# Dilated attention in a two-layer encoder block: probabilities transposed in place, and scores placed behind the next projection

## The chip, the cores and the metric

The kernel runs on one core of one Trainium2 chip. The metric is the device time of one execution in microseconds; lower is better. A core has a matrix engine (TensorE, PE in the profile), three engines for elementwise work (VectorE = DVE, ScalarE = ACT, GpSimd = POOL), an engine that here only issues DMAs (SyncE = SP), 16 DMA engines, an on-chip memory of 128 partitions (SBUF) and a matrix accumulator of eight banks (PSUM).

## The reference, cut to what matters

One batch of 512 tokens, width 1024, float32, 16 heads of 64. Layer A is a dilated attention of three groups of heads (dilations 1, 4 and 16; each query sees 64, 64 and 16 keys of its residue class on either side), whose outputs are weighed by their softmax denominators; one softmax over all keys of the three groups is the same. Layer B is a neighbourhood attention on an 8 x 64 grid.

```python
def mixer_a(hn, w_in, w_out, q_gain, k_gain, t5_bias):
    proj = hn @ w_in
    qkv = proj[..., :n_qkv].reshape(b, s, 3, 3, N_HEADS, HEAD_DIM)
    gate = proj[..., n_qkv:]
    for g, (window, dilation) in enumerate(((128, 1), (512, 4), (2048, 16))):
        q = rms_norm(qkv[:, :, g, 0], q_gain[g])
        k = rms_norm(qkv[:, :, g, 1], k_gain[g])
        v = qkv[:, :, g, 2]
        o, lse = dilated_group_attention(q, k, v, t5_bias[g], dilation, (window // 2) // dilation)
    alpha = softmax(lses)
    y = sum(alpha * outs) * silu(gate)
    return y @ w_out

# per layer: x = x + mixer(rms_norm(x))
```

## The kernel before

**Tiling and stages.** `main()` runs, for each of eight pairs of heads of layer A (`hc` 0 to 7; the text calls the pairs heads 0 to 7), three projections: `rawk` (k of the groups 1 and 2, and their v), `rawq` (q of all groups and k of group 0), each 96 matmuls of 128 x 512, and the pair of `v0_a` and `gate_a` with 24 each. Head 7 takes `rawq` ahead of `rawk`, and the gate of head 6 comes behind them. Then come the output product of layer A, eight heads of layer B, and the output product of B. A float32 product is three products of rounded parts: weights are split by ACT into `wh` (L127) and by DVE or POOL into `wl` (L131; POOL takes two of five). Weights are loaded on SP's queue into three buffers `wraw`.

**Order.** The order of PE is written out by hand: `run(main(), side())` walks the projections (main) and lets the attention work (side) in between, by a clock that counts PE time. `yield "wait", key, delay` in the side work means: not before `delay` ns of that clock after the stamp `key`; `yield n` means n ns on; `later_on` sets a timer for DMAs. The order on the other engines, and that of DMAs not held by `keep_in_program_order`, is chosen by the scheduler of the framework, from its own estimate of times.

**A head of layer A.**
- `project_qk`: ACT evacuates each of four accumulators (L444, L468 for the first head), POOL squares (L268), DVE sums (L269), the norm's inverse root is computed in 14 small operations on POOL for `rawk` and 11 on DVE for `rawq` (`rsqrt`, L108 to L120), and DVE scales in place (L290). `rawq` is then transposed on DVE in 32 x 32 blocks (`turn_q`, L519).
- `k_a`: two groups of PE transposes of `rawk` (L505 and on).
- `q_a`: `rawq` goes to DRAM in four writes and comes back in four reads (k0, q0 and the two parts of q12), by timers at 0 and 6.8 us. The writes have rows of 512 bytes. Then `split_q` (L552) makes k0h (ACT, L559), q0h (ACT, L578), q0l (DVE, L580) and k0l (DVE, L561).
- `scores(u)`, in two halves u of two query tiles t each: per half four PSUM banks `log` (two tiles x two heads), out of a pool `side` of four. Group 0 is three products of 192 or 256 columns into the front half of a bank, the groups 1 and 2 are 64 small products into its back half.
- `softmax` (L741): per bank two sweeps of DVE that add the bias and keep the minimum (scores are negated): one over group 0 (L748), one over the groups 1 and 2 that starts from the first one's minimum (L759). Then ACT's exponential with the sum (L770), DVE's reciprocal (L608), ACT's scaling (L609), into a tile `p` of four buffers.
- `turner.put` (L681): DVE transposes p in 32 x 32 blocks into a tile `tr` of one buffer; `turner.send`: four writes to DRAM (L690) and four reads (L694) finish the transpose into `pq` ("pt" in the profile). Head 7 transposes on PE instead (`turn_p`, L774).
- `weigh`: the product with v (`o`, 24 matmuls), whose result is gated by `put_y` into y_h (ACT, L635) and y_l (POOL, L636).

**Where these stand on PE before.** The scores of a head 1 to 5 follow its own projections: first half, then (waiting for rawk of the next head) the product with v of the head before, and 10 us behind that rawk the second half. Head 0's halves wait for rawk and rawq of head 1. Head 6's follow each other by 11 us during rawq and rawk of head 7.

The lines that set these places:

```python
def k_a(hc):
    yield "wait", ("rawk", hc), 12500 if hc == 0 else 25500 if hc == 1 else 18500 if hc < NHC - 1 else 10000

def q_a(hc):
    yield "wait", ("rawq", hc), 15000 if hc != 1 else 18000

def land():
    yield "wait", ("rawq", hc), 27000 if hc != 1 else 30000
```

Of the kernel before, what the change touches and what calls it, by code (L numbers as in the profile page):

```python
# [42 lines left out]
def tile_hybrid_encoder(  # L43
# [45 lines left out]
    ones = cp.tile([P, S], F32R, name="ones")  # L89
# [176 lines left out]
    def squares(v, ss, i, ns):  # L266
        sq = wk.tile([P, 512], F32, tag="sq", name="sq")[:, : ns * 64]
        nc.gpsimd.tensor_mul(sq.rearrange("p (c r) -> p c r", r=32) if ns == 8 else sq, v, v)  # L268
# [6 lines left out]
    def head_norm(raw, ss, ns, held):  # L275
# [5 lines left out]
        def scale():  # L281
            for i in range(4):
                by = rs[:, i * ns : (i + 1) * ns].unsqueeze(2)
                if ns == 8:
                    v = raw[:, :, i, :].rearrange("p (a b) r -> p a b r", b=2)
                    by = by.unsqueeze(3).to_broadcast([P, ns, 2, 32])
# [62 lines left out]
    for _ in range(9):  # L349
        nc.tensor.matmul(busy, ones[:, :P], ones, start=True, stop=True)  # L350
# [61 lines left out]
    pq = wk.tile([P, 4096], F32, tag="pt", name="pt", bufs=1)  # L412
    rk = wk.tile([P, 4608], F32, tag="rawk", name="rawk", bufs=1)
# [4 lines left out]
    def project_qk(n, ns, key, hc, guard, first=False, **kw):  # L418
# [3 lines left out]
        def evac(i, acc):  # L422
# [11 lines left out]
            if key == "rawq":  # L434
                pieces = [(raw[:, :, i, :], acc.rearrange("p (c r) -> p c r", r=32))]
# [69 lines left out]
    def k_a(hc):  # L505
        yield "wait", ("rawk", hc), 12500 if hc == 0 else 25500 if hc == 1 else 18500 if hc < NHC - 1 else 10000
# [14 lines left out]
    def q_a(hc):  # L521

        yield "wait", ("rawq", hc), 15000 if hc != 1 else 18000
        raw = st.pop(("rawq", hc))
        d = dr.tile([16, 32, 4, P], F32, name="qd", tag="qd", bufs=2)
        q12 = wk.tile([P, 2, 512], F32, tag="q12", name="q12", bufs=1)
        k0, q0 = (wk.tile([P, 512], F32, tag="eg", name="q0") for _ in range(2))
        lands, left = ((3, k0), (0, q0), (1, q12[:, 0, :]), (2, q12[:, 1, :])), [4]

        def write(t):  # L530
            src = raw[32 * t : 32 * t + 32].rearrange("k c i r -> k c (i r)")
            tc.keep_in_program_order(nc.sync.dma_start(d[:, :, t, :].rearrange("c k x -> k c x"), src))
            if t == 3:
                stamp["q", hc] = 0

        def read(f, dst):
            src = d[4 * f : 4 * f + 4].rearrange("a k t x -> (a k) (t x)")
            tc.keep_in_program_order(nc.sync.dma_start(dst, src))
            left[0] -= 1

        for n in range(4):
            later_on(700 * n, partial(write, n))
            later_on(6800 + 700 * n, partial(read, *lands[n]))
        def land():
            yield "wait", ("rawq", hc), 27000 if hc != 1 else 30000
            assert not left[0]
            st["q", hc] = split_q(q0, k0, q12)
            yield
# [3 lines left out]
    def split_q(q0, k0, q12):  # L552
# [4 lines left out]
        src = k0.rearrange("p (t j r) -> p t r j", t=4, j=4)  # L557
        trj4 = lambda t: t[:, 64:EXT].rearrange("p (t r j) -> p t r j", t=4, j=4)
        nc.scalar.copy(trj4(k0h), src)  # L559
        put_k([(q0h, q0l, q0)], 0)  # L560
        nc.vector.tensor_sub(trj4(k0l), src, trj4(k0h.bitcast(F32)))  # L561
        return q0h, q0l, q12, k0h, k0l
# [107 lines left out]
    class turner:  # L670
# [3 lines left out]
        def __init__(self, run):  # L674
            self.run, self.left = run, 4
            self.t = wk.tile([P, 2048], F32, tag="tr", name="tr", bufs=1)
# [24 lines left out]
    def attn_a(hc):  # L701
        e0, e12 = st.pop(("e", hc))
        q0h, q0l, q12, k0h, k0l = st.pop(("q", hc))
# [5 lines left out]
        def scores(u):  # L709
# [13 lines left out]
            for t, lgs, cs, n in tiles:  # L723
                for g in range(2):
                    for j in range(4):
                        c = P * t + 32 * j
                        for hd in range(2):
# [3 lines left out]
                                q12[hs, g, c : c + 32],  # L731
# [8 lines left out]

        def softmax(hd, t, lg, cs, n):  # L741
            pr = wk.tile([P, 512], F32, tag="p", name="p", bufs=4)
            mn = wk.tile([P, 4], F32, tag="mn", name="mn", bufs=4)
            if t == 0:
                nc.gpsimd.memset(pr[:, 0:64], 0.0)
            if t == 3:
                nc.gpsimd.memset(pr[:, 192:256], BIG)
            nc.vector.tensor_tensor_reduce(  # L748
                out=pr[:, cs : cs + n],
                in0=lg[:, cs : cs + n],  # L750
                in1=e0[:, hd, cs : cs + n],
                scale=1.0,
                scalar=3.0e38,
                op0=ALU.add,
                op1=ALU.min,
                accum_out=mn[:, 0:1],
            )
            v = lambda t_: t_[:, 256:512].rearrange("p (g c) -> p g c", g=2)
            nc.vector.tensor_tensor_reduce(  # L759
                out=v(pr),  # L760
                in0=v(lg),
                in1=e12[:, 2 * hd : 2 * hd + 2, 96 - 32 * t : 224 - 32 * t],
                scale=1.0,
                scalar=mn[:, 0:1],
                op0=ALU.add,
                op1=ALU.min,
                accum_out=mn[:, 1:2],
            )
            row = pr[:, cs:512]
            nc.scalar.activation(row, row, AF.Exp, bias=mn[:, 1:2], scale=-1.0, accum_out=mn[:, 2:3])  # L770
            normalise(row, mn)
            return pr

        def turn_p(hd, t, pr):  # L774
            tp = bank("tp")
            for i in range(4):
                transpose(tp[:, i * P : (i + 1) * P], pr[:, i * P : (i + 1) * P])
# [3 lines left out]
        def weighed():  # L781

            yield "wait", ("rawk", hc + 1), 0
# [456 lines left out]
```

## Time and profile before

| what | value |
|---|---|
| time, median of 3 runs | 869.8 us (869.4 to 869.89) |
| the profiled execution | 867.95 us, of it 866.1 us span |
| TensorE (PE) | mean granted clock 0.992 of full speed |
| weights, activations and probabilities moved | 145.43 MB, mean 168 GB/s |

The page of the profile shows one execution: the busy time of each engine as a share of the span, the span in 40 slices, DMA queues, the chain of work that ended last, and the costliest groups of instructions. Further views of the same trace are used: the list of waits (engine, line, what released it: total us, times, longest), timelines (start, duration, engine, line, operation, out<-in, form; in brackets the idle time before it and what ended it), windows (engine busy times in a stretch of the span, then clock, DMA share and GB/s) and groups of instructions of one form (busy us, mean ns | idle before). For groups of operations such as "x64", one row stands for several instructions in a run.

### The profile page before, as it was taken

Reading aid. Unit: us, or ns where it says so; the run is one execution under the profiler, and the core shown is the slowest. Engines: PE = TensorE matmul, PEld = TensorE weight load, DVE = VectorE, ACT = ScalarE, POOL = GpSimd, SP = SyncE. Lnnn points to the kernel's source line nnn. Section 1 sums busy time; section 2 is a strip of 40 time slices with the busy share of each in tenths; the row PEclk is TensorE's granted clock in tenths of the full one; section 3 lists DMA queues with packets and bytes.
Section 4 is the critical chain, followed back from the end, with each engine's and each line's share of the span. In section 5 each row is a group of like instructions: output and inputs, shape, how many; then the busy total and the mean of one; then the engine's idle time right before and its main releaser. Section 6 shows DMA issues by size and latency. Waiting matters only on the chain.

```text
span 866.1 us, 15411 instructions
## 1 busy us (share of the span) xinstructions
PE 845.2 (98%) x5515; PEld 702.3 (81%) x5515; DVE 520.8 (60%) x1339; ACT 433.1 (50%) x924; POOL 304.9 (35%) x493
## 2 busy tenths in 40 slices
PE   9999998999999999999998988999999999999998
PEld 7788886788787788788787876789988999889786
DVE  7355583765674665665664855538576656766643
ACT  7434552653553553553553464436366545665541
POOL 2342432441541541541542332111444345533511
PEclk9999999899999999999999999999999999999999
DMA  6355468379478479478469196255235654556223
GB/s 246 111 158 175 147 190 232 133 204 231 139 209 241 139 193 239 137 203 231 138 173 262 49 256 183 64 180 194 80 119 155 172 169 147 153 165 182 98 91 128
DMA packets 81212, 145.43 MB, mean 168 GB/s; under 512 B 7408, under 2 KB 41136, under 8 KB 81136
## 3 DMA queue, kind: packets, MB, share of 16 engines
q1 hardware_dynamic: 80848, 144.44, 56.7%
q8 instruction: 43, 0.70, 0.4%
q14 instruction: 33, 0.27, 0.1%
q10 hardware_dynamic: 288, 0.01, 0.0%
HBM read 111.20 MB, written 33.22 MB: 167 GB/s over the span
## 4 chain that ended last, share of the span: by engine, by line
PE 76%; DMA 9%; DVE 5%; ACT 4%; POOL 3%; issue 1%; SPq 1%; ACTq 0%; DVEq 0%; POOLq 0%
PE acc L206 64%; PE log L206 4%; PE o L206 4%; DMA wraw<-in_w 3%; DMA q<-qd 3%; PE tp L210 3%; DMA qd<-rawq 1%; DMA e<-l_d 1%; POOL wl L131 1%; POOL sq L268 1%; DVE rawq L519 1%; DVE rawq L290 1%; DMA pt<-td 1%; ACT wh L127 1%; ACT rawq L444 1%
## 5 line engine op out<-in xcount | busy, mean ns | idle before, releaser
L206 PE MATMUL acc<-wh,hn_h 128*128 128x512 f32 (+1 forms) x768 | 293.3, 382 | 4.4 <-ACT rawq L444 2.4
L127 ACT CAST wh<-wraw 128x512 fp32r<-128x512 f32 (+1 forms) x276 | 161.1, 589 | 251.4 <-PE acc L206 190.8
L206 PE MATMUL acc<-wl,hn_h 128*128 128x512 f32 (+1 forms) x768 | 285.4, 372 | 0.6 <-DVE wl L131 0.6
L206 PE MATMUL acc<-wh,hn_l 128*128 128x512 f32 (+1 forms) x768 | 285.6, 372 | 0.0
L131 POOL TENSOR_TENSOR wl<-wraw,wh 128x512 fp32r<-128x512 f32 (+1 forms) x110 | 141.1, 1283 | 389.5 <-ACT wh L127 367.2
L131 DVE TENSOR_TENSOR wl<-wraw,wh 128x512 fp32r<-128x512 f32 (+1 forms) x166 | 116.8, 704 | 116.2 <-ACT wh L127 111.9
L206 PEld LDWEIGHTS acc<-wh,hn_h 128*128 128x128 f32 x768 | 144.4, 188 | 33.4 <-issue 4.0
L206 PEld LDWEIGHTS acc<-wh,hn_l 128*128 128x128 f32 x768 | 144.3, 188 | 20.6
L206 PEld LDWEIGHTS acc<-wl,hn_h 128*128 128x128 f32 x768 | 144.5, 188 | 20.0 <-DVE wl L131 0.9
L206 PE MATMUL acc<-hn_h,wh 128*128 128x512 f32 x192 | 78.6, 409 | 2.6 <-ACT rawk L444 2.3
L206 PE MATMUL acc<-hn_l,wh 128*128 128x512 f32 x192 | 75.8, 395 | 0.0
L206 PE MATMUL acc<-hn_h,wl 128*128 128x512 f32 x192 | 75.8, 395 | 0.0
L770 ACT ACTIVATE p<-p,mn 128x512 f32<-128x512 f32 (+1 forms) x64 | 45.1, 705 | 59.9 <-DVE mn L759 59.9
L609 ACT ACTIVATE p<-p,mn 128x512 f32<-128x512 f32 (+3 forms) x128 | 69.4, 593 | 2.9 <-DVE mn L608 2.9
L269 DVE TENSOR_REDUCE ss<-sq 128x4 f32<-128x256 f32 (+1 forms) x96 | 48.4, 505 | 29.2 <-POOL sq L268 28.7
L268 POOL TENSOR_TENSOR sq<-rawk 128x256 f32<-128x256 f32 x64 | 42.7, 675 | 64.9 <-ACT rawk L444 51.9
L681 DVE STREAM_TRANSPOSE tr<-p 128x512 f32<-128x512 f32 (+1 forms) x80 | 53.7, 683 | 10.4 <-ACT p L609 6.2
L206 PE MATMUL acc<-y_h,wh 128*128 128x512 f32 x128 | 52.2, 408 | 0.0
L206 PE MATMUL acc<-y_h,wl 128*128 128x512 f32 x128 | 50.0, 391 | 0.0
L206 PE MATMUL acc<-y_l,wh 128*128 128x512 f32 x128 | 50.0, 390 | 0.0
L206 PEld LDWEIGHTS acc<-hn_h,wh 128*128 128x128 f32 x192 | 36.9, 192 | 13.0 <-ACT rawk L444 4.9
L206 PEld LDWEIGHTS acc<-hn_h,wl 128*128 128x128 f32 x192 | 36.6, 191 | 8.0
(130 smaller groups left out, 1075.8 us busy)
## 6 DMA issues: line engine op xcount, KB each, us to landing
wraw<-in_w SPq DMA_DIRECT2D x95, 512.0 KB
wraw<-in_w SPq DMA_DIRECT2D x38, 384.0 KB
td<-tr SPq DMA_DIRECT2D x56, 256.0 KB
pt<-td SPq DMA_DIRECT2D x56, 256.0 KB
qd<-rawq SPq DMA_DIRECT2D x32, 256.0 KB
q<-qd SPq DMA_DIRECT2D x32, 256.0 KB
td<-tr SPq DMA_DIRECT2D x24, 224.0 KB
pt<-td SPq DMA_DIRECT2D x24, 224.0 KB
```

What stands on the lines that cost most here:

```text
L127: nc.scalar.copy(h, raw)
L131: eng.tensor_sub(l, raw, h.bitcast(F32))
L206: nc.tensor.matmul(o, l, r, **kw)
L210: nc.tensor.transpose(o, i, ident)
L268: nc.gpsimd.tensor_mul(sq.rearrange("p (c r) -> p c r", r=32) if ns == 8 else sq, v, v)
L269: nc.vector.tensor_reduce(ss[:, i * ns : (i + 1) * ns], sq.rearrange("p (a b) -> p a b", b=64), axis=AX.X, op=ALU.add)
L290: m = nc.vector.tensor_mul(v, v, by)
L444: nc.scalar.activation(dst, src, AF.Copy, scale=rs_n[:, i : i + 1])
L519: nc.vector.transpose(raw[:, :, i, :], raw[:, :, i, :])
L609: nc.scalar.activation(pr, pr, AF.Copy, scale=mn[:, 3:4])
L681: nc.vector.transpose(dst, src[:, :n].rearrange("p (i b k) -> p i b k", b=4, k=32))
L770: nc.scalar.activation(row, row, AF.Exp, bias=mn[:, 1:2], scale=-1.0, accum_out=mn[:, 2:3])
```

## The change

What it does, by parts:

1. **Softmax and transposition.** A tile `uu` of 4096 columns replaces `p` and `tr`. `spot` gives every (head, t) its place in it, each half of the scores its own 2048 columns, for heads 0 to 6 ("far") already laid out as the DRAM writes want it. The sweeps write there: four of 128 columns per bank (group 0 in two pieces, groups 1 and 2), each starting from the minimum so far, in place of two. Masked corners of tiles 0 and 3 are set to a large number, so that the exponential runs over all 512 columns. DVE transposes p where it lies, and `turner.send` writes from `uu`. Layer B takes slots of `uu` in turn.
2. **Order on PE.** The scores of heads 0 to 6 wait for the end of the next head's first projection; then come `split_q`, the pending product with v, the first half 1.2 us later and the second half 4.5 us of projection behind that. The functions for the old places go.
3. **q.** `rawq` is kept in another order of its 32-column blocks, so that the DRAM writes have rows of 2 KB, and the reads bring one quarter of the partitions each, all groups at once, into one tile `qt`. The waits of `k_a`, `q_a` and `land` are 19.5, 15.5 and 28 us. k0h is held in program order.
4. **Warm-up.** `ones` is two columns wide and broadcast.

```diff
-    ones = cp.tile([P, S], F32R, name="ones")
+    ones = cp.tile([P, 2], F32R, name="ones")
...
+    uu = wk.tile([P, 4096], F32, tag="uu", name="uu", bufs=1)
+    p_slots = cycle(range(4))
+    def p_slot():
+        o = 512 * next(p_slots)
+        return uu[:, o : o + 512]
...
-                pieces = [(raw[:, :, i, :], acc.rearrange("p (c r) -> p c r", r=32))]
+                src = acc.rearrange("p (f a r) -> p f a r", f=4, a=4)
+                pieces = [(raw[:, :, i, :].rearrange("p (a f) r -> p f a r", a=4), src)]
...
-        yield "wait", ("rawk", hc), 12500 if hc == 0 else 25500 if hc == 1 else 18500 if hc < NHC - 1 else 10000
+        yield "wait", ("rawk", hc), 12500 if hc == 0 else 19500 if hc < NHC - 1 else 10000
...
-        yield "wait", ("rawq", hc), 15000 if hc != 1 else 18000
+        yield "wait", ("rawq", hc), 15500
...
+        d = dr.tile([4, P, 512], F32, name="qd", tag="qd", bufs=2)
+        qt = wk.tile([P, 4, 4, P], F32, tag="q12", name="qt", bufs=1)
...
+        def write(a):
+            src = raw[:, 4 * a : 4 * a + 4].rearrange("p f i r -> p (f i r)")
+            tc.keep_in_program_order(nc.sync.dma_start(d[a], src))
...
+        def read(a):
+            dst = qt[32 * a : 32 * a + 32].rearrange("k t f x -> k t (f x)")
+            src = d[a].rearrange("(t k) x -> k t x", t=4)
+            tc.keep_in_program_order(nc.sync.dma_start(dst, src))
...
-            yield "wait", ("rawq", hc), 27000 if hc != 1 else 30000
+            yield "wait", ("rawq", hc), 28000
...
-        nc.scalar.copy(trj4(k0h), src)
-        put_k([(q0h, q0l, q0)], 0)
+        tc.keep_in_program_order(nc.scalar.copy(trj4(k0h), src))
+        by_t = lambda t: t.rearrange("p (t x) -> p t x", t=4)
+        put_k([(by_t(q0h), by_t(q0l), qt[:, :, 0, :])], 0)
...
+        far = hc < NHC - 1
+        def spot(hd, t):
+            o = 256 * hd + 128 * (t % 2) if far else 1024 * (t % 2) + 512 * hd
+            return 2048 * (t // 2) + o, *((32, 512) if far else (128, 32))
...
         def softmax(hd, t, lg, cs, n):
-            pr = wk.tile([P, 512], F32, tag="p", name="p", bufs=4)
...
+            least = 3.0e38
+            for i in range(4):
+                b, nb = {(0, 0): (2, 2), (3, 1): (0, 2)}.get((t, i), (0, 4))
+                c, w = P * i + 32 * b, 32 * nb
+                by = e0[:, hd, c : c + w] if i < 2 else e12[:, 2 * hd + i - 2, 96 - 32 * t : 224 - 32 * t]
+                bk = lambda t_: t_.rearrange("p (b k) -> p b k", k=32)
+                nc.vector.tensor_tensor_reduce(
+                    out=sb(uu, o + i_ * i + b_ * b, [[b_, nb], [1, 32]]),
+                    in0=bk(lg[:, c : c + w]),
+                    in1=bk(by),
+                    scale=1.0,
+                    scalar=least,
+                    op0=ALU.add,
+                    op1=ALU.min,
+                    accum_out=mn[:, i : i + 1],
+                )
+                least = mn[:, i : i + 1]
+            row = sb(uu, o, [[512, 4], [1, 128]] if far else [[1, 512]])
+            nc.scalar.activation(row, row, AF.Exp, bias=least, scale=-1.0, accum_out=mn[:, 4:5])
+            normalise(row, mn[:, 2:6])
...
             for u in range(2):
-                if u == 0 and hc:
-                    yield 600
-                elif hc == 0:
-                    yield "wait", ("rawk" if u == 0 else "rawq", 1), 0
-                elif hc < NHC - 2:
-                    yield "wait", ("rawk", hc + 1), 10000
-                else:
-                    yield 11000
-                turned = turner(512)
+                yield 1200 if u == 0 else 4500
+                turned = turner(uu[:, 2048 * u : 2048 * u + 2048], 512)
                 turners.append(turned)
                 for hd, t, pr in scores(u):
-                    turned.put(pr, 512, 256 * hd + 128 * (t % 2))
-                later_on(7500, partial(turned.send, pq[:, 2048 * u : 2048 * u + 2048], 11000, 1500))
-                if 0 < hc < NHC - 2 and u == 0:
-                    yield from weighed()
+                    nc.vector.transpose(pr, pr)
+                later_on(9500, partial(turned.send, pq[:, 2048 * u : 2048 * u + 2048], 11000, 1500))
...
-                if hc == NHC - 2:
-                    yield "wait", ("rawq", hc + 1), 0
+
+                follow = ("rawk" if hc < NHC - 2 else "rawq"), hc + 1
+                yield "wait", follow, 0
+                yield from st.pop(("land", hc))
+                if pending:
                     pending.pop(0)()
-                yield from chain(st.pop(("land", hc)), attn_a(hc))
+                yield from attn_a(hc)
```

More of the change, by code (lines that the diff above doesn't have):

```diff
@@ L349, in tile_hybrid_encoder @@
     for _ in range(9):
-        nc.tensor.matmul(busy, ones[:, :P], ones, start=True, stop=True)
+        wide = lambda n: ones[:, 0:1].to_broadcast([P, n])
+        nc.tensor.matmul(busy, wide(P), wide(S), start=True, stop=True)
     wsteps = steps()
@@ L702, in attn_a @@
         e0, e12 = st.pop(("e", hc))
-        q0h, q0l, q12, k0h, k0l = st.pop(("q", hc))
+        q0h, q0l, qt, k0h, k0l = st.pop(("q", hc))
         k12, v12 = st.pop(("k12", hc))
@@ L744, in softmax @@
             if t == 0:
[L745 removed]
+                nc.gpsimd.memset(sb(uu, o, [[b_, 2], [1, 32]]), BIG)
             if t == 3:
[L747 to L770, printed above, removed]
@@ L778, in turn_p @@
             dst = sb(pts[0], at(t, 0, hd, 0), [[32, 4], [512, 4], [1, 32]])
             nc.vector.tensor_copy(dst, tp.rearrange("p (i a r) -> p i a r", i=4, a=4))
-        def weighed():
-            yield "wait", ("rawk", hc + 1), 0
-            pending.pop(0)()
-            yield
         def weigh():
@@ L830, in attn_a @@
             for u in range(2):
-                if u == 0:
-                    yield "wait", ("gate", hc), 500
                 yield 600
@@ L836, in attn_a @@
                 if pending:
-                    yield "wait", ("gate", hc - 1), 16800
+                    yield "wait", ("gate", hc - 1), 15500
                     pending.pop(0)()
@@ L1006, in softmax @@
         def softmax(hd, u, lg):
-            pr = wk.tile([P, 512], F32, tag="p", name="p", bufs=4)
+            pr = p_slot()
             for b in (2 * u, 2 * u + 1):
```

63 lines of the change are left out of this document (30 added, 33 removed).

## The prediction

> **What bounds the kernel now.** I read the page first: the busy shares of the engines, then the list of what TensorE (PE) waited for.
>
> ```profile
> span 866.1 us, 15411 instructions
> PE 845.2 (98%) x5515; PEld 702.3 (81%) x5515; DVE 520.8 (60%) x1339; ACT 433.1 (50%) x924; POOL 304.9 (35%) x493
> ```
>
> ```profile
> PE log L206 <- ACT q0h L578: 4.2, 1, 4.2
> PE tp L210 <- DVE rawk L290: 3.1, 1, 3.1
> PE acc L206 <- ACT rawq L444: 2.4, 1, 2.4
> PE acc L206 <- ACT rawk L444: 2.3, 1, 2.3
> PE acc L206 <- ACT gt L478: 1.8, 2, 1.6
> ```
>
> PE is busy for 98% of the span and its matmuls are the same before and after (the order of the built instructions has equal counts). So the change can give back only what PE now waits for, and can cost only by new waits. Five entries hold 13.8 us (each row: total, times, longest), in three places: 4.2 in head 1, 1.8 between projections, 7.8 in heads 6 and 7. To a wait belongs the clock that is lost behind it; the PE timeline has the resuming instructions, the windows the granted clock (the third number from the end).
>
> ```profile
> 151.48 0.53 PE L206 MATMUL log<-k0h,q0h 64*128 64x192 f32 x2 [4.22 <-ACT q0h L578]
> 168.66 0.39 PE L206 MATMUL log<-k0h,q0h 64*128 64x256 f32 x2
> 170.64 0.50 PE L206 MATMUL acc<-wh,hn_h 128*128 128x512 f32 x1
> 186.00 0.39 PE L206 MATMUL acc<-hn_h,wh 128*128 128x512 f32 x1
> 186.23 0.39 PE L206 MATMUL acc<-hn_l,wh 128*128 128x512 f32 x1
> 476.34 1.97 PE L206 MATMUL o<-pt,rawk 128*64 128x128 f32 x32
> 479.97 0.50 PE L206 MATMUL acc<-wh,hn_h 128*128 128x512 f32 x1
> 508.11 0.80 PE L206 MATMUL acc<-hn_h,wh 128*128 128x512 f32 x1 [2.33 <-ACT rawk L444]
> ```
>
> ```profile
> 150.00:160.00 10.00, 8.47 (x119) 6.83 (x121) 7.00 (x27) 7.00 (x18) 3.98 (x5) 0.69 0.26 90
> 470.00:480.00 10.00, 7.60 (x66) 5.53 (x64) 4.39 (x6) 5.04 (x8) 4.52 (x4) 1.00 0.43 145
> 500.00:510.00 10.00, 7.67 (x31) 5.97 (x30) 6.06 (x20) 8.79 (x22) 2.45 (x6) 0.89 0.81 234
> 520.00:530.00 10.00, 6.90 (x25) 4.97 (x24) 6.10 (x10) 1.89 (x4) 3.14 (x8) 0.83 0.90 288
> ```
>
> From 150 on, a mean of 0.69 is 6.2 us at half speed, so until 156.2; PE resumed at 151.48, and 4.7 us at half lose 2.4. Head 1's wait thus costs 4.2 + 2.4 = 6.6. The 2.4 in 470:480 cost no clock (1.00). In 500:510, 0.89 is 2.2 us at half before 510 and some behind it: I take 1.5 lost, 3.8 with its wait. In 520:530, 0.83 is 3.4 us at half, 1.7 to 2.3 lost: 5.1 with the 3.1. Heads 6 and 7 together: 2.4 + 3.8 + 5.1 = 11.3. All losses: 6.6 + 1.8 + 11.3 = 19.7.
>
> Three lengths are read off starts: a 512-column matmul takes 0.23 (186.00 to 186.23), a half's group of scores 1.98 (168.66 to 170.64), the product with v 3.63 (476.34 to 479.97).
>
> **The change part by part.** R is the moment at which the projection that the scores now wait for ends (rawk of the next head; for head 6, rawq of head 7).
>
> *Removed: head 1's wait (-6.6) and the gate's (-1.8).* In the built order, from the end of rawq of head 1 to its first score stand 153 projection matmuls and a product with v; before, 138 and a group of scores. That is 15 x 0.23 + 3.63 - 1.98 = 5.1 more, less two small transposition groups (estimated 0.3 each): 4.5. The q write is also due at 15.5 us behind rawq, not 18.0. 4.5 + 2.5 = 7.0 exceeds 4.2, so q is there. The writes and reads of q stay four each; the reads now land in one tile. SP's order has changed: the next weights' loads stand ahead of the reads of transposed p, so their copies are earlier and p is later; p is needed only behind the next rawk, some 96 matmuls (22 us) on, which covers it. -8.4; bound 0 if SP's queue holds q up by the 7.0.
>
> *Added in every head: eight more sweeps per half.* Each tile's minimum is taken in four sweeps of 128 columns in place of two.
>
> ```profile
> 350.22 0.35 DVE L748 CUSTOM_DVE_ANT_0 p<-log,e 128x192 f32<-128x192 f32 x1
> 350.49 0.48 DVE L759 CUSTOM_DVE_ANT_1 p<-log,e,mn 128x256 f32<-128x256 f32 x1
> 350.90 0.48 DVE L759 CUSTOM_DVE_ANT_1 p<-log,e,mn 128x256 f32<-128x256 f32 x1
> 351.31 0.42 DVE L748 CUSTOM_DVE_ANT_0 p<-log,e 128x256 f32<-128x256 f32 x1
> 351.65 0.42 DVE L748 CUSTOM_DVE_ANT_0 p<-log,e 128x256 f32<-128x256 f32 x1
> ```
>
> Start to start: 0.27 for 192 columns, 0.34 for 256, so 0.07 for 64 and 0.20 for 128; the form with a running minimum takes 0.41 at 256, so 0.28 at 128. Four first and twelve later sweeps: 4 x 0.20 + 12 x 0.28 = 4.2 a half; before 2.9. Bounds: 0.20 each (3.2), or 0.41 each whatever the width, since the new output is scattered in rows of 32 (6.6). I take 4.2: width shows in the rows. DVE time itself is covered (60% busy); what counts is when a half's four score banks come free for the next half.
>
> *Moved: scores behind the next rawk.* They now meet that projection's norm on ACT, POOL and DVE.
>
> ```profile
> 507.23 3.01 ACT L444 ACTIVATE rawk<-acc,rs_n 128x256 f32<-128x256 f32 x8
> 358.66 0.20 POOL L109 TENSOR_SCALAR rs<-nv 128x16 int32<-128x16 int32 x1
> 359.85 0.23 POOL L120 TENSOR_TENSOR rs<-rs,na 128x16 f32<-128x16 f32 x1
> 360.33 1.59 POOL L636 TENSOR_TENSOR y_l<-gt,y_h 128x512 fp32r<-128x512 f32 x1
> 362.06 1.29 POOL L131 TENSOR_TENSOR wl<-wraw,wh 128x512 fp32r<-128x512 f32 x1
> 362.19 1.70 DVE L131 TENSOR_TENSOR wl<-wraw,wh 128x512 fp32r<-128x512 f32 x1 [1.87 <-ACT wh L127]
> 365.49 1.43 DVE L290 TENSOR_TENSOR rawk<-rawk,rs 128x256 f32<-128x256 f32 x4 [1.59 <-POOL rs L120]
> L559 ACT CAST k0h<-q 128x512 fp32r<-128x512 f32 x8 | 9.0, 1121 | 36.1 <-DMA q<-qd 36.1
> L561 DVE TENSOR_TENSOR k0l<-q,k0h 128x512 fp32r<-128x512 f32 x8 | 8.9, 1107 | 56.0 <-ACT k0h L559 56.0
> ```
>
> ACT evacuates until R + 1.3 (eight in 3.0, most of them during rawk). A copy of weights (0.6 by the page's 589 ns) and k0h (1.1) follow: R + 3.0. k0l on DVE: R + 4.1. The last squares and their sums end near R + 2.2. POOL then has 14 small operations of 0.3 (four steps from 358.66 to 359.85 take 1.19) and half a microsecond of hand-overs: R + 6.8. DVE's scaling of rawk takes 1.4: R + 8.2. But POOL goes straight on to y_l (1.6), and 362.19 is a DVE subtraction of a usual 0.70 that took 1.70, ending only behind the POOL operation started at 362.06. So the scaling ends between R + 8.2 and R + 9.5. In the built DVE order the first half's sixteen sweeps follow it: R + 12.4 to 13.7. On PE the second half's scores stand at R + 13.1 and need their third bank at R + 13.6. Slack: 1.2 to -0.1. I charge 0.25 to each of heads 1, 3, 4 and 5: +1.0 (bounds 0 and 6).
>
> The Trainium skill ("SBUF — State Buffer", "Who interferes with whom") says that a DVE operation with two SBUF operands and a POOL operation lock each other out for a whole instruction, and one with an operand in PSUM is free of it. The row 362.19 agrees; by the rule the sweeps, which read scores from PSUM, would keep their 4.2 beside POOL, and the scaling would always pay y_l, putting the slack at its lower end and the sum some 1 us up.
>
> *Head 2.* In the built order POOL gets, inside the same chain, a small preparation of layer B:
>
> ```profile
> 234.68 0.83 POOL L404 TENSOR_SCALAR rp<-rp 128x248 f32<-128x248 f32 x1
> ```
>
> With it two small ones (estimated 0.7 together) and y_l (1.6) come before the chain's last step: 3.1 late against a slack of about 0.5, so 2.6 and 0.6 of clock: +3.2 (bounds 0 and 5).
>
> *Head 0.* No product with v is pending, so the first scores stand at R + 2.0 while k0h comes at 3.0 and k0l, used by the second of the three products, at 4.1: 2.0 waited. Its second half stands at R + 9.5, with the scaling between its sweeps: 0.7. +2.7 (bounds 0 and 3.3).
>
> *Heads 6 and 7: 11.3 becomes 6.5.* The three old waits were head 7's q projection, scores of 6 and k projection colliding.
>
> ```profile
> 486.60 2.49 DVE L290 TENSOR_TENSOR rawq<-rawq,rs 128x512 f32<-128x512 f32 x4
> 490.50 2.49 DVE L519 STREAM_TRANSPOSE rawq<-rawq 128x512 f32<-128x512 f32 x4
> L770 ACT ACTIVATE p<-p,mn 128x512 f32<-128x512 f32 x48 | 34.5, 719 | 38.2 <-DVE mn L759 38.2
> ```
>
> Now scores of 6 start at R + 7.7, the second half at R + 15.1. On DVE the first half's sweeps share the stretch with scaling and transposes of rawq (5.0): 7.7 + 1 + 4.2 + 5.0 is R + 18, so a bank wait of 3.0, with a clock loss of 1.7 as in 520:530. Then rawk of 7 is evacuated behind four exponentials (4 x 0.72, of which 1.1 covered): 1.8. Sum 6.5; -4.8 (bounds -11.3, and +1 if each collision returns).
>
> The Trainium skill ("TensorE: Matmul & The Clock Gate", "Why this matters for your kernels") asks for no PE gaps above about 3 us. Here 2.33 already halved the clock (0.89) while 2.40 did not (1.00), so the measurement decides; by the rule the bank waits of 3.0 and below would lose no clock and the sum would be 2.3 lower.
>
> *Head 7* has its halves close together and 2 x 1.3 more sweeping: +0.7, most of it under the pending product with v of 3.6; uncovered 2.6.
>
> *Nothing:* the narrow `ones` in the warm-up; the relaid rawq (same sizes); transposing p in place (same instruction, other address); layer B's slots (its PE order is unchanged). Cover for all is DVE's, ACT's and POOL's idle 40% and more.
>
> **Sum:** -6.6 - 1.8 + 1.0 + 3.2 + 2.7 - 4.8 + 0.7 = -5.6. The profiled execution took 867.95, so 862.3; the median of the runs shown, 869.8, lies 1.85 above it: 864.
>
> **The rivals.**
>
> *All waits go.* Every new wait finds its cover (the scaling meets a free POOL, sweeps at 3.2): 867.95 - 19.7 + 1.85 = 850. For it: the removed waits are single events, and the slack is positive by most rows. Against: k0h after rawk's evacuation in head 0, and heads 6 and 7, where DVE is asked for 10 us in 7.
>
> *A bank wait in every head: slower.* The place: the second half's third score group, waiting on the first half's last sweeps. If scattered sweeps cost 0.41 flat, a half takes 2.4 more; with slack 0.5 each of heads 1 to 5 then waits about 2, and as 2.33 did, pays up to 1.5 of clock: 3.5 x 5 = 17 on top of 864: 881. It decides from 1.4 us a head (5.6 / 5 and the 0.25 charged), first sweeps ending behind R + 15. For it: the scaling's row shows a POOL collision, and sweeps of 32-element pieces appear nowhere in the trace. Against: sweeps' time follows their width.
>
> *It comes to the same.* The waits of heads 6 and 7 only change places (11.3 stays): 864 + 4.8 = 869. Also what it comes to if q lands no earlier than before and half a term is lost with it.
>
> **How the numbers follow.** Forecast 0.47 (858 to 868, its own range), all waits go 0.14, bank waits 0.28, the same 0.11. A measurement of this kernel tells about 0.2% (1.7 us) from no change; so faster 0.47 + 0.14 = 0.61, same 0.11, slower 0.28. The range leaves half of the first rival below 851 and rather under half of the second above 878.
>
> **What would show it.** Right: the list of PE waits loses q0h, gt and rawq; a wait of `log` on the sweeps (line 775) appears, largest in heads 2 and 6, and one on k0h in head 0; sweeps follow each other at 0.20 to 0.28; the clock stays at 1.0 around 150 and 510; DVE's busy time rises by some 16 x 1.3 = 21 us. Wrong: sweeps at 0.4, a `log` wait in every head, rawk's scaling ending later than R + 9.5, or q still late in head 1.

## The result and the profile after

| | before | after |
|---|---|---|
| median of 4 runs | 869.61 us (869.4 to 869.89) | 925.72 us (923.64 to 931.09) |
| ratio | | 1.0654 (95% interval 1.0608 to 1.0701) |
| profiled execution, of it span | 867.95, 866.1 us | 924.81, 922.9 us |

The changed kernel is 6.5% slower: 56 us. First the page's span and first line, then the top of the list of what PE waited for (total us, times, longest us):

```profile
span 922.9 us, 15706 instructions
PE 863.4 (94%) x5515; PEld 713.0 (77%) x5515; DVE 541.1 (59%) x1595; ACT 434.7 (47%) x924; POOL 300.6 (33%) x493
```

```profile
PE acc L206 <- ACT rawk L458: 32.3, 6, 7.2
PE tp L210 <- DVE rawk L295: 4.3, 1, 4.3
PE log L206 <- DVE mn L775: 3.3, 1, 3.3
```

PE has the same 5515 matmuls, yet its busy time rose by 863.4 - 845.2 = 18.2 us, and its idle time from 20.9 to 59.5, by 38.6: together the 56.8 by which the span grew. The 18.2 go with the halved clock behind the waits: a mean clock of 0.992 before and 0.969 after loses some 7 and 29 us over the spans, in part while PE was idle anyway. Most of the added idle time is one entry, 32.3 us after against 2.3 before: a projection that cannot start since ACT has not evacuated `rawk`. Five of its six waits stand once in each of heads 1 to 5, at one place: between the next head's rawk and its rawq, just ahead of where the scores now stand.

Followed back from one of them (head 1), in the timelines of PE, ACT, SP, DVE and POOL of the changed kernel:

```profile
157.38 0.39 PE L206 MATMUL acc<-wh,hn_l 128*128 128x512 f32 x1
164.96 0.80 PE L206 MATMUL acc<-wh,hn_h 128*128 128x512 f32 x1 [7.19 <-ACT rawk L458]
```

```profile
162.94 0.72 ACT L594 ACTIVATE q0h<-qt,gk 128x512 fp32r<-128x512 f32 x1 [9.95 <-DMA qt<-qd]
163.57 0.60 ACT L127 CAST wh<-wraw 128x512 fp32r<-128x512 f32 x1
164.08 3.02 ACT L458 ACTIVATE rawk<-acc,rs_n 128x256 f32<-128x256 f32 x8
```

```profile
146.48 1.80 SPq L545 DMA_DIRECT2D qd<-rawq  x4
...
150.73 1.77 SPq L552 DMA_DIRECT2D qt<-qd  x3
```

```profile
145.17 1.29 DVE L533 STREAM_TRANSPOSE rawq<-rawq 128x512 f32<-128x512 f32 x2
```

```profile
121.71 3.16 POOL L270 TENSOR_TENSOR sq<-rawq 128x512 f32<-128x512 f32 x3 [0.53 <-ACT rawq L458]
124.83 1.29 POOL L131 TENSOR_TENSOR wl<-wraw,wh 128x512 fp32r<-128x512 f32 x1
133.68 0.23 POOL L768 MEMSET uu<- 128x64 f32 x2 [7.56 <-DMA td<-uu]
133.87 1.04 POOL L270 TENSOR_TENSOR sq<-rawq 128x512 f32<-128x512 f32 x1
```

Read from the end: POOL's fill of the masked corners waited 7.56 us until p's writes to DRAM had left the room (`td<-uu`). Behind it stood the last of the four squares of rawq; the norm, scaling and transposes of rawq followed on DVE until 146.5, then q's write and read. ACT came to q0h at 153 and stood there for 9.95 us, with the evacuation of the next rawk queued behind it, and PE stood 7.19 us for that.

In head 3 the scheduler had put the fill behind the square, and PE waited 3.2 us instead of 6.6 to 7.2 (the resuming matmul stands at 308.25). That is one head; a_memset below, with the fill behind the square in every head, repeats it only in part. The POOL timeline of head 3:

```profile
274.97 1.04 POOL L270 TENSOR_TENSOR sq<-rawq 128x512 f32<-128x512 f32 x1
280.47 0.23 POOL L768 MEMSET uu<- 128x64 f32 x2 [4.45 <-DMA td<-uu]
```

### The profile page after: what moved, and what is told of

The parts are those of the page before. It is cut to its first block, busy times and chain, and to the rows that moved or that the text cites. A ratio compares the mean times of both kernels' runs of the same rounds, so it can differ in the third digit from the quotient of the medians.

```text
span 922.9 us, 15706 instructions
## 1 busy us (share of the span) xinstructions
PE 863.4 (94%) x5515; PEld 713.0 (77%) x5515; DVE 541.1 (59%) x1595; ACT 434.7 (47%) x924; POOL 300.6 (33%) x493
## 4 chain that ended last, share of the span: by engine, by line
PE 49%; DMA 23%; DVE 13%; ACT 7%; issue 3%; POOL 2%; SPq 2%; ACTq 0%; POOLq 0%; DVEq 0%
PE acc L206 40%; DMA qt<-qd 9%; DMA td<-uu 7%; PE o L206 4%; DVE uu L775 4%; PE log L206 3%; DMA wraw<-in_w 3%; ACT uu L787 3%; DMA qd<-rawq 3%; DMA pt<-td 2%; PE tp L210 2%; DVE wl L131 2%; ACT uu L625 2%; ACT rawk L458 1%; DVE rawq L533 1%
## 5 line engine op out<-in xcount | busy, mean ns | idle before, releaser
L206 PE MATMUL acc<-wh,hn_h 128*128 128x512 f32 (+1 forms) x768 | 296.5, 386 | 33.4 <-ACT rawk L458 32.3
L206 PE MATMUL acc<-wl,hn_h 128*128 128x512 f32 (+1 forms) x768 | 288.5, 376 | 3.1 <-DVE wl L131 3.0
L131 POOL TENSOR_TENSOR wl<-wraw,wh 128x512 fp32r<-128x512 f32 (+1 forms) x110 | 138.9, 1263 | 393.7 <-ACT wh L127 368.4
L625 ACT ACTIVATE uu<-uu,mn 128x512 f32<-128x512 f32 (+2 forms) x128 | 69.9, 599 | 0.1
L787 ACT ACTIVATE uu<-uu,mn 128x512 f32<-128x512 f32 x64 | 45.8, 717 | 31.9 <-DVE mn L775 31.9
L775 DVE CUSTOM_DVE_ANT_0 uu<-log,e,mn 128x128 f32<-128x128 f32 (+1 forms) x192 | 54.8, 339 | 0.0
L596 DVE SCALAR_TENSOR_TENSOR q0l<-qt,gk,q0h 128x512 fp32r<-128x512 f32 x8 | 6.0, 750 | 69.0 <-ACT q0h L594 65.1
L829 DVE STREAM_TRANSPOSE uu<-uu 128x512 f32<-128x512 f32 x56 | 38.8, 703 | 10.8 <-ACT uu L625 10.8
```

The lines of the kernel that those rows point to most:

```text
L131: eng.tensor_sub(l, raw, h.bitcast(F32))
L206: nc.tensor.matmul(o, l, r, **kw)
L625: nc.scalar.activation(pr, pr, AF.Copy, scale=mn[:, 3:4])
L775: nc.vector.tensor_tensor_reduce(out=sb(uu, o + i_ * i + b_ * b, [[b_, nb], [1, 32]]), in0=bk(lg[:, c : c + w]), in1=bk(by), scale=1.0, sc ...
L787: nc.scalar.activation(row, row, AF.Exp, bias=least, scale=-1.0, accum_out=mn[:, 4:5])
L829: nc.vector.transpose(pr, pr)
```

## The experiments

Three parts of the change were taken one by one: the order on PE, p in place with room of its own, and the new trip of q. Two pins were added to them: the fills, and q0h, held in program order. "Ratio" is to the kernel before on the same chip; the rounds ran on different chips, on which the kernel before took 869.6 to 872.8 us, so that small differences between rounds are read from the ratios. Every row has the narrow `ones`, and every row with the new order or the new trip holds k0h in program order.

| kernel | order | in place | new q | pins | us | ratio |
|---|---|---|---|---|---|---|
| p_only | | x | | | 914.4 | 1.050 |
| b_newq | | | x | | 908.8 | 1.046 |
| o_oldq | x | | | | 907.0 | 1.040 |
| a_oldq | x | x | | | 910.4 | 1.048 |
| o_only | x | | x | | 925.3 | 1.063 |
| changed | x | x | x | | 925.7 | 1.065 |
| p_memset | | x | | fills | 879.4 | 1.007 |
| p_newq | | x | x | fills | 916.9 | 1.053 |
| a_oldq_ms | x | x | | fills | 890.9 | 1.026 |
| a_memset | x | x | x | fills | 915.5 | 1.052 |
| a_q0h | x | x | x | q0h | 906.3 | 1.041 |
| o_both | x | | x | both | 887.6 | 1.018 |
| a_oldq_both | x | x | | both | 881.6 | 1.014 |
| a_both | x | x | x | both | 879.6 | 1.008 |

**First round: two links of the chain, two parts.** The pins are

```diff
+            i = nc.scalar.activation(dh, src, AF.Copy, scale=gk[:, g : g + 1])
+            if g == 0:
+                tc.keep_in_program_order(i)
...
+                tc.keep_in_program_order(nc.gpsimd.memset(sb(uu, o, [[b_, 2], [1, 32]]), BIG))
```

The first is a_q0h, the second (with its twin for tile 3) a_memset.

> The changed kernel with q0h held in program order on ACT, so behind the evacuation of rawk and behind k0h. Theory (q arrives late, and q0h ahead of the evacuation on ACT turns that into PE waits): the 32.3 us of `acc` waiting for the evacuation go, and some 12 us of half clock with them; q is as late as before, so each of heads 1 to 5 waits 1 to 3 us at its scores instead: 885 to 898 us. Rival (the lateness of q is the whole cost, wherever it is waited for): the waits only move to the scores, 915 to 925 us.

> The changed kernel with the fills of the masked corners held in program order on POOL, so behind the norm of rawk instead of ahead of the last square of rawq. Theory (the fill waits for the writes of p to DRAM that read the same room, and the last square of rawq stands behind it): the last square comes about 8 us earlier in heads 1, 2, 4 and 5, and with it q; their PE waits fall from 7 to the 3.2 us that head 3 has, where the fill already stands behind: 900 to 910 us. Rival (q is late because the transfers of both halves, q and the weights fill the DMA engines at once): q lands as late, 920 us or more.

Measured: 906.3 and 915.5 us, both slower than the theory and faster than the rival. In a_q0h the 32.3 us at the evacuation are gone but for 0.4, but POOL still stands behind the fill, and PE now waits 9.6 us for weights' splits (`acc` on `wl`): 4.0 for one on POOL, 5.6 for those on DVE (3.0 in the changed kernel). In a_memset the fill no longer holds the squares, but the waits at the evacuation hardly change:

```profile
PE acc L206 <- ACT rawk L458: 30.5, 6, 8.1
```

They fell in heads 2 and 5 (3.0 and 4.6 us) and grew in heads 3 and 4 (7.7 and 8.1). Counted from the last matmul of rawq, the last transpose ends 7.0 us earlier in head 1 (16.9, not 23.9), but q0h begins only 2.2 us earlier (38.2, not 40.4): the rest was lost on the way through DRAM, which from the end of the last transpose takes 16.7 to 22.8 us in heads 1 to 5 of a_memset and 15.9 to 18.1 in the changed kernel. So by itself this pin does not shorten the waits to head 3's 3.2; its 10.2 us come mostly from smaller waits elsewhere, as at rawk of head 7 (4.3 to 1.0), and the clock behind them.

> The new order on PE and the new path of q, but probabilities in p and transposed into tr, one buffer, with two sweeps per bank as before the change. Theory: the fills do not wait for DMA any more, but the second half's transposes wait on DVE until the first half's writes have left tr, 7.5 us of projection behind it, with weights' splits queued behind them: slower than the changed kernel, 930 to 980 us. Rival (the fill's wait was the only new one): about 905 us.

> The old order on PE and the old path of q, but the new softmax: four sweeps, in place, room of its own for each half. Theory (in place costs 1.3 us of DVE a half, which is covered, and the fills find the room long free, since the halves are far apart): within 4 us of 870. Rival (the scattered sweeps or the fills cost by themselves): 880 or more.

o_only keeps p in four buffers with one `tr` (the loop is the changed one, with `turned = turner(512)` and `turned.put`); p_only keeps the old loop with the new softmax. Measured: 925.3 and 914.4. The theory fell in both; in p_only the rival came, in o_only neither case. p_only was to be free, but in the old order too, in heads 2 to 5, the fill stands ahead of the last square. Its POOL timeline, in head 3:

```profile
275.32 0.24 POOL L761 MEMSET uu<- 128x64 f32 x2 [8.74 <-DMA td<-uu]
275.52 1.04 POOL L268 TENSOR_TENSOR sq<-rawq 128x512 f32<-128x512 f32 x1
```

And o_only, whose fills go into `p`, which no DMA reads, has 39.4 us at the evacuation of rawk: its fills wait for a transpose into `tr`, which waits for the writes out of `tr`, and all four squares of rawq stand behind them.

**Second round: both pins, the fills alone in the old order, p's traffic.** a_nop is a_memset with `turned.left = 0` in place of the timer for `send`, and a constant put into `pq` once; a_both_late gives the second half's reads, in heads 0 to 5, 28 us after its writes instead of 11.

> Both pins at once on the changed kernel: q0h behind the evacuation of rawk on ACT, the fills behind the norm of rawk on POOL. If the two links are independent, the gains add (19.4 and 10.2 off 925.7): 894 to 899 us. If the saturated DMA engines set when q lands, the earlier squares gain little once nothing but the scores waits for q: 899 to 906 us.

> The changed kernel with the fills pinned (as a_memset, 915.5 us), and the trip of p through DRAM left out in heads 0 to 6: the product with v reads a constant, so layer A's output is not the reference's; PE does the same work. It takes 4 MB a head off the DMA engines. Theory (q lands late because p's transfers of both halves now fill the engines just ahead of q): q lands about 10 us earlier, before q0h's turn on ACT, and the waits of acc for the evacuation go though q0h still stands ahead of it: 855 to 872 us. Rival (q's own new path, 2 KB rows and reads into a quarter of the partitions, is slow): 900 us or more.

> p_only (old order, new softmax in place, 914 us) with the fills pinned on POOL behind what was issued before them. Theory (all that in place costs in the old order is the fill ahead of the last square of rawq): 866 to 875 us. Rival (the four scattered sweeps, or writing from the room itself, cost too): 885 us or more.

> a_both with the DRAM reads of the second half's p moved by 17 us, so that they stand behind q's write and mostly behind its reads on SP's queue. Theory (transfers are served in the order of issue by full engines, so q waits for p's reads ahead of it): q lands some 4 us earlier, 8 to 15 us under a_both, unless p then comes late for the product with v. Rival (q's lateness is the DVE chain of rawq's norm and not its place in the queue): the same as a_both within 4 us.

Measured: 879.6, 888.5, 879.4 and 906.5; none of the four lies in a range given for it. The pins gain more together (46.1) than their sum (29.6). In a_both's trace the waits for POOL's splits are gone. ACT still waits for q's reads (18.3 us at k0h), but in heads 0 to 5 PE loses at most 1.5 us a head to q0h and q0l: the rest of q's lateness falls into slack that the new order has. In the old order the fill was all but 0.7% of what p in place costs. Taking p's traffic away gave 27.0 us against a_memset, and q's way from the last transpose to q0h then takes 14.5 to 15.7 us in heads 1 to 5, not 16.7 to 22.8. So p's transfers lengthen q's trip, but they are not all: 8.8 us at the evacuation stayed. Whether it is their place or their amount that counts, a_nop does not tell, since it takes both away. a_both_late does not test its theory: p itself came late (PE waits of `o` on p's reads 24.0 us, on a weights load 10.1).

**Third round: the trip of q, and versions that might beat both.** p_newq is p_memset with the new q; b_h1 is the kernel before with one edit, p_h1 p_memset with the same; a_both2 is a_both with other gaps in head 6.

```diff
-        yield "wait", ("rawq", hc), 15000 if hc != 1 else 18000
+        yield "wait", ("rawq", hc), 15000
...
-            yield "wait", ("rawq", hc), 27000 if hc != 1 else 30000
+            yield "wait", ("rawq", hc), 27000
...
-                yield 1200 if u == 0 else 4500
+                yield (1200 if u == 0 else 4500) if hc < NHC - 2 else (4500 if u == 0 else 4500)
```

> p_memset (old order, in place, fills pinned; 879.4 us) with the new path of q: rawq in its new order, writes of 2 KB rows, reads by quarters into qt, waits 15.5 and 28 us. If the new path carries q faster by itself, head 1's wait of 7.9 us shrinks and the time falls to 868 to 874 us. If it is no faster, 877 to 884. If it is slower than the old one (whose reads are spread over all partitions), waits on q0h appear in heads 2 to 5 too: 890 or more.

> The kernel before with one edit: in head 1 the due times of q's trip are those of the other heads (15 and 27 us, not 18 and 30). Theory of the prediction (head 1's 4.2 us of waiting and 2.4 of clock come from the late start of the trip): 6 to 7 us faster than before, about 863. Rival (DMA engines are full there, so the start is not what is late): within 2 us of before.

> p_memset with the same edit in head 1. p_memset waits 7.9 us there, with some 3 of clock behind; if the start sets it, 870 to 875 us; if not, 877 to 882.

> a_both (879.6 us) with head 6's product with v and first half 3.3 us of projection later. Its PE waits for q0h, q0l, the o bank and the first half's banks there, 7.1 us in all, with some 5 of clock: if q is only late by that much, these shrink and the time falls to 870 to 876 us; if what follows comes late in its turn (head 7), it stays at 878 to 882.

Measured: 916.9 (the third case of three), 871.2 (ratio 1.0011, interval 0.9991 to 1.0032), 883.5 and 885.9. In the old order the new trip of q costs about what the fill costs there (37.6 and 35.0 us). An earlier due time does not start q's write in head 1 any earlier: before, the last transpose ends at 133.28 and the write begins at 133.31, in b_h1 at 134.93 and 134.96. q0h then begins 2.2 us earlier, counted from the start of rawq's evacuation (38.2, not 40.4), but the edit moves the scores too, by 3 us, so that the wait there was 5.4 us in b_h1's profile, 4.2 before. p_h1 and a_both2 end above the worse of their two cases. Nothing here beats the kernel before.

**Fourth round: the parts alone and the table filled.** b_newq is the kernel before with the trip of q alone; the three whose names begin with a_oldq are the changed kernel, a_memset and a_both with the old trip; o_oldq is the new order alone; o_both is o_only with both pins.

> The kernel before with only the new path of q (its order of blocks, 2 KB rows, reads by quarters of the partitions into qt, its waits). Theory (reads into a quarter of the partitions take longer, so k0h and q0h come 4 us later, and the scores of each head wait 4 to 5 us with 2 of clock): 895 to 910 us, with waits of log on k0h and q0h in heads 1 to 5. Rival (the new path costs only where p's transfers collide with it, in place): 868 to 876 us.

> The changed kernel with the old path of q (512-byte rows out, whole-partition reads back), everything else as changed. Theory (the fill makes q late by 8 us whatever its path, the path adds 4 more): the waits of acc on the evacuation fall from 7 to about 3 us a head: 900 to 912 us. Rival (the engines are saturated, so the path does not matter): 920 or more.

> a_memset (915.5 us) with the old path of q. Theory: q 4 us or more earlier than in a_memset, where q0h is read 5 us behind the end of rawk; acc waits 0 to 2 us a head: 875 to 890 us. Rival (saturated engines): 905 or more.

> a_both (879.6 us) with the old path of q: with q there in time, the small waits at the scores (q0h, q0l; 0.3 to 1 us a head) and the 2.8 us in head 6 go: 866 to 875 us. Rival (a_both's remaining 10 us over before lie in heads 6 and 7, not in q): 877 to 881.

> The new order on PE alone: old path of q, p and tr as before, two sweeps per bank. Theory (both halves' transfers of p now stand just ahead of q's, tr holds the second half's transposes and with them the fills): q late by itself, waits of acc on the evacuation of 3 to 5 us a head: 895 to 915 us. Rival (the order alone is harmless): 860 to 872 us.

> o_only (925.3 us) with both pins, q0h on ACT and the fills on POOL. If the pins are all that is needed, it comes to a_both's 879 to 882 us without room of its own; if the one buffer tr matters, the second half's transposes wait on DVE for the first half's writes, with rawq's norm behind them, and it stays at 890 to 910.

Measured: 908.8, 910.4, 890.9, 881.6, 907.0 and 887.6. The first two, o_oldq and (by 0.9 us) nearly a_oldq_ms came as the theory had it (though the last waits 1.2 to 4.6 us a head, not 0 to 2); in a_oldq_both, but for 0.6 us, its rival did. With both pins the old trip is no faster than the new: 881.6 and 879.6 us, ratios 1.014 and 1.008 with intervals that meet. o_both lies between its two cases, 8 us above a_both: that is what p in place, with room of its own, brings once the pins are in. In its list of what DVE waited for, the transposes into the one buffer stand for 42.9 us:

```profile
DVE tr L692 <- DMA td<-tr: 42.9, 7, 7.8
```

**How the three parts meet.** In head 2, counted in us from the last matmul of rawq, taken from each trace:

| kernel | last square begins | last transpose ends | first copy of q or k0 begins | next rawk's last matmul |
|---|---|---|---|---|
| before | 3.4 | 17.8 | 27.7 | 35.4 |
| p_only | 11.4 | 24.0 | 34.4 | 43.5 |
| b_newq | 3.4 | 17.8 | 33.0 | 41.5 |
| o_oldq | 7.7 | 21.8 | 35.1 | 33.1 |
| changed | 9.6 | 22.2 | 38.3 | 33.1 |
| a_memset | 3.4 | 17.8 | 34.5 | 33.1 |
| a_oldq_ms | 3.9 | 17.0 | 32.7 | 33.1 |

q has one path, rawq's norm, its transposes, the write, the read, ACT's copy, and each part lengthens it: in place by 8 us ahead of the last square, the new trip by 5.3 behind the last transpose, the new order by 4 ahead of the square (there the fills wait for `tr`) and 3 or more in the transfers. In the old order the scores wait for that; in the new one q0h stands ahead of the evacuation, so that all of it beyond some 33 us is a stop of the projections. Head 2 is the mildest for a_memset: in its heads 1, 3 and 4 q0h begins at 38 to 40, in the changed kernel's at 35 to 40.

For the trip, the queue of SP in b_newq and before, and the ACT row that ends it:

```profile
215.86 1.80 SPq L538 DMA_DIRECT2D qd<-rawq  x4
217.77 0.69 SPq L175 DMA_DIRECT2D wraw<-in_w  x1
218.57 0.59 SPq L545 DMA_DIRECT2D qt<-qd  x1
222.81 0.33 SPq L175 DMA_DIRECT2D wraw<-in_w  x1
223.23 1.33 SPq L545 DMA_DIRECT2D qt<-qd  x3
```

```profile
231.01 1.06 ACT L567 CAST k0h<-qt 128x512 fp32r<-128x512 f32 x1 [4.21 <-DMA qt<-qd]
```

```profile
203.58 3.35 SPq L532 DMA_DIRECT2D qd<-rawq  x4
207.04 0.86 SPq L175 DMA_DIRECT2D wraw<-in_w  x1
210.22 0.81 SPq L538 DMA_DIRECT2D q<-qd  x2
...
213.46 1.14 ACT L559 CAST k0h<-q 128x512 fp32r<-128x512 f32 x1 [4.38 <-DMA q<-qd]
```

The last read is issued 8.7 us (224.56 - 215.86) and 8.9 us (212.45 - 203.58) behind the first write: no difference. But k0h before needs only the first of the four reads (k0, whole), and now all four (a quarter of the partitions of each group): 231.01 is 6.4 us behind the end of the last issue, 213.46 is 3.2 behind the start of the first. And the reads by quarters move slower, by the DMA view of two stretches of 3 and 2 us in which reads of q run beside one load of weights, p_newq from 228 and before from 277:

```profile
DMA packets 369, 0.70 MB, mean 234 GB/s; under 512 B 45, under 2 KB 45, under 8 KB 369
...
q1 hardware_dynamic: 369, 0.70, 100.5%
```

```profile
DMA packets 330, 0.70 MB, mean 349 GB/s; under 512 B 32, under 2 KB 32, under 8 KB 330
...
q1 hardware_dynamic: 330, 0.70, 93.2%
```

234 GB/s against 349, with the DMA engines (the last number, the share of 16) full or nearly so in both. The Trainium skill ("SBUF — State Buffer", "Door 1: The DMA port swizzle (why `[64,N]` ≈ `[32,N]`)") has partitions 0 to 31 reach 8 of SBUF's 16 ports, and 189 against 328 GB/s for transfers of 1 MiB. Some weights move in these stretches, so the two ratios (1.5 and 1.7) are not to be compared closely; the direction agrees. That the ports are the cause, and how the 5.3 us divide between the slower reads and the wait for all four, no run here shows.

For the order, windows of 10 us over about one head, first the changed kernel, then before (the last two numbers are the share of the DMA engines and GB/s):

```profile
241.00:251.00 10.00, 10.00 (x128) 7.69 (x127) 4.75 (x18) 2.23 (x3) 7.22 (x19) 0.87 0.30 100
251.00:261.00 10.00, 10.00 (x112) 8.06 (x111) 8.94 (x52) 6.43 (x14) 2.08 (x2) 1.00 0.28 99
...
281.00:291.00 10.00, 10.00 (x47) 8.28 (x47) 8.43 (x14) 3.58 (x6) 2.51 (x2) 1.00 0.97 245
291.00:301.00 10.00, 10.00 (x45) 8.26 (x44) 1.39 (x2) 2.50 (x4) 1.98 (x2) 1.00 1.04 325
```

```profile
225.00:235.00 10.00, 10.00 (x115) 7.76 (x112) 4.41 (x8) 5.76 (x11) 7.34 (x17) 1.00 0.47 152
235.00:245.00 10.00, 10.00 (x49) 8.27 (x49) 7.06 (x28) 6.31 (x14) 2.88 (x9) 1.00 0.54 165
245.00:255.00 10.00, 10.00 (x46) 8.26 (x45) 6.42 (x10) 5.66 (x10) 6.68 (x6) 1.00 0.90 239
255.00:265.00 10.00, 8.39 (x38) 6.64 (x37) 8.32 (x21) 2.24 (x4) 1.79 (x2) 1.00 1.01 250
265.00:275.00 10.00, 10.00 (x47) 8.23 (x48) 5.10 (x9) 3.50 (x6) 1.48 (x2) 1.00 0.91 230
```

The same bytes are moved (145.4 MB both); but the engines now run at 0.3 for 20 us behind rawk, until p's first half is ready, and are full for the 20 us ahead of q's landing (q0h begins at 306.23). Before, they are as full for the 30 us ahead of it (k0h begins at 278.52), and at 0.5 before that. So full engines ahead of q are not new; what the windows show as new is the slack lost behind rawk. That p's transfers cost q time in the new order rests on a_nop.

## Why the prediction was wrong, by its own steps

- **"Nothing: ... transposing p in place (same instruction, other address)"** is the step that failed first along the chain of the wait. The DVE work is the same, but the room is now what the DMA reads from, so the next head's first writer of it waits for a transfer, and that writer is not the sweep but the fill, a small operation on POOL with a square of rawq queued behind it. In the old order that costs 35 us, 4.3 points of the ratio (p_only against p_memset). In the changed kernel the same pin is worth 10.2 us alone, and 26.7 where q0h is out of the evacuation's way (906.3 - 879.6).
- **"so q is there"**, the -8.4, and **"The writes and reads of q stay four each"**: the count stayed and what each brings changed. b_newq alone: 38.9 us. Of the 7.0 us by which q was to gain in head 1, the 2.5 of the due time were never there: the write starts at the end of the last transpose, before and after (133.28 and 133.31; 146.46 and 146.48). The rival "q lands no earlier" was priced at half a term.
- **"ACT evacuates until R + 1.3 ... and k0h (1.1) follow"**: true of k0h, which the change pins. q0h, the other copy from the same reads, is in no term of the sum; it was not pinned, and the built order has it ahead of the evacuation. Its place is worth 925.7 - 906.3 = 19.4 us alone and, with the fills pinned, 915.5 - 879.6 = 35.9 us: of the two pins the larger part, and the nearest cause of the 32.3 us at the evacuation. The scaling of rawk, which was to end by R + 9.5, ended in head 1 at 175.9, 18 us behind R.
- **p's DMAs**, which the moved scores take along, were looked at for whether p comes late, not for who shares the engines with it. o_oldq: 37 us, in which both of the last two points meet, and fills that wait for `tr`.
- The losses of heads 6 and 7 were expected to shrink from 11.3 to 6.5. Head 6 now waits for q0h (2.3), for q0l (0.9), for the `o` bank (1.9) and for its own banks (3.3), and 4.3 stands at rawk of head 7: 12.7 us of idle time against 7.8 before, no gain. The forecast of one of these, the bank wait, was 3.0.
- Right, but small: the sweeps follow each other as their widths gave, 0.18 to 0.21 for the first of a bank (0.20 forecast) and 0.27 for the later ones (0.28), by DVE's timeline below, and DVE's busy time rose by 20.3 us where 21 were forecast. Head 0's scores waited for k0h and k0l for 1.26 + 0.71 = 2.0, as forecast. No bank wait came in heads 1 to 5, the mechanism of the rival to which the chances of "slower" were given: the kernel became slower, but not by it. These sizes were right; the sum was of the wrong rows. Head 1's old wait at `log` is gone from the list, but not its reason: q is late there still, and the 7.19 us at the evacuation stand in its place.

```profile
111.11 0.25 DVE L775 CUSTOM_DVE_ANT_0 uu<-log,e 128x128 f32<-128x128 f32 x1
111.29 0.29 DVE L775 CUSTOM_DVE_ANT_0 uu<-log,e 128x128 f32<-128x128 f32 x1
111.50 0.35 DVE L775 CUSTOM_DVE_ANT_0 uu<-log,e,mn 128x128 f32<-128x128 f32 x1
111.77 0.35 DVE L775 CUSTOM_DVE_ANT_0 uu<-log,e,mn 128x128 f32<-128x128 f32 x1
```

The three parts' costs alone (44.2, 38.9 and 36.8 us over before on the same chip) add to twice what they cost together; that they lengthen one path fits this, as the table of head 2 has it. What stays open: how the 36.8 of the new order divide between the fills (which there wait for `tr`), p's transfers and q0h's place; why a_memset's trip is longer in heads 1, 3 and 4 than the changed kernel's; and the 6.7 us that a_both has over before on the same chip, which lie mostly in heads 6 and 7 by the trace, where the one try at them (a_both2) went the wrong way.

## What to carry to other kernels

Follow a change of buffer by its new last reader: where that is a DMA, ask which engine's instruction first writes the room again, and what is queued behind it. Where the order of an engine is chosen by a scheduler, read in the built order the place of every instruction that waits for a transfer, not of the one that the change pins, and ask who stands behind it if the transfer is 10 us late. And a trip through DRAM is as long as the last read that its first user needs.

## What was not expected of the hardware

The clock does not follow the length of one wait alone: in the changed kernel the waits of 1.26 and 0.71 us in head 0, 1.1 us apart and 4 us behind one of 1.56, were followed by a stretch at half clock (0.72 over 95 to 101), where before the change a single wait of 2.40 was not (1.00 over 470 to 480). PE's timeline and the window:

```profile
95.42 0.36 PE L206 MATMUL log<-k0h,q0h 64*128 64x192 f32 x2 [1.26 <-ACT k0h L574]
96.49 0.36 PE L206 MATMUL log<-k0l,q0h 64*128 64x192 f32 x2 [0.71 <-DVE k0l L577]
```

```profile
95.00:101.00 6.00, 4.86 (x81) 3.86 (x82) 2.87 (x10) 0.57 (x2) 3.69 (x14) 0.72 0.28 90
```

In b_newq the write of q by rows of 2 KB was issued in 1.80 us on SP's queue, by rows of 512 bytes in 3.35: the issue is shorter, and it bought nothing: the last read is issued as late as before, and the reads set the end of the trip.
